# Keys of six running streams turned in 32x32 blocks on VectorE, their scores by matmuls on small parts of the array

## The chip, the core and the metric

One Trainium2 chip, of which one core is used. The metric is the device time of one execution in microseconds, from the first to the last instruction with what the runtime counts around it. A core has TensorE (matmul, PE; its weight loads are listed as PEld), VectorE (DVE), ScalarE (ACT), GpSimd (POOL) and SyncE (SP), which here issues nearly all DMAs.

## The reference, cut to what matters

One step of a two-layer encoder in fp32: a prompt of 1024 rows and eight running streams of 16 rows each, model width 1024. Layer 0 joins a gated linear recurrence (four heads) with differential attention (four heads, two components of 64 columns each, so 128 columns a head); layer 1 is a pooling mixer; each layer ends in a ConvFFN. The change touches the attention of the running streams alone. Each of the eight streams has 2048 cached keys and values for each head, and its 16 new rows attend to those and to its own 16 new keys:

```
def probs(qa, ka):
    s = einsum('bqhd,bkhd->bhqk', qa, ka) * scale + bias
    return softmax(where(visible, s, neg))
attn = probs(q[..., :64], k[..., :64]) - lam * probs(q[..., 64:], k[..., 64:])
out = einsum('bhqk,bkhd->bqhd', attn, v)
```

For one stream the scores are a 128 x 2064 matrix: 4 heads x 2 components x 16 rows down, keys across.

## The kernel before, in words

The kernel is one long program in which side work, written as a Python generator, is woven into main work: `weave(main, side, per_step, skip)` takes `per_step` steps of the side for each step of the main, after the first `skip`. A step is what lies between two `yield`s. Every engine works through its own instructions in order; the framework adds the waits between engines and gives out buffers, among them eight PSUM banks of 2 KB a partition (`bank`) shared by all. It can also place an instruction earlier than the text has it.

Stages in order of time: column groups of the input projection with prompt attention beside them; then, from about 357 to 597 us, four feature-major groups (`fm_group`, tile pfm, 18 steps each) and the token-major group "ag" (`tm_group`, tile ptm, 18 steps) with the running streams (`streams`) beside them at R3 = 1.924 from the sixth step on (S3 = 5); then six stream steps alone (S4) and the recurrence (`hgrn`) with stream steps at R4 = 0.553; then the output projection's first columns with the rest of the streams at R5 = 1.669. The ConvFFN of layer 0, the pooling mixer and the ConvFFN of layer 1 fill the rest to 2590 us.

`streams` goes through n = 0, 1, 2, ...; group n is 256 cached keys, b = n // 8 is the stream and g = n % 8 the group in it. For each n it has up to four steps:

- `key_load` of group n + 1 (512 KB, three buffers kraw), and `key_tr` of group n: eight 128x128 transposes on TensorE into two banks (pk), copied to kt by VectorE and ScalarE, one each.
- `key_scores` of group n - 1: four matmuls, one for each head, each with 32 columns of queries (two components of 16; `qbd` has zeros where a component does not look) against 256 keys, into one bank (pss), which is copied to Sx. The four heads lie in four strips of 32 output partitions. Behind a stream's last group follows its `softmax`.
- `prob_tr` of group n - 11: two transposes of probabilities (ppt), copied to pT, and the load of 512 KB of values (vraw, three buffers).
- `prob_values` of group n - 12: eight matmuls of 32 columns of probabilities against 128 columns of values, summed in one bank (pos) over the whole stream. The stream's own 16 keys and values go through psn and vn.

So a step in which n is below 11 has the first two parts alone. In the profile a matmul in fp32 of 128x32 weights has two records, a transpose one, and their weight loads likewise. Projection matmuls are three for each product, over operands split into two parts; in pfm each streams 384 columns.

After the fm stage `more_act` makes ScalarE take all of the streams' copies.

## Time and profile before

| | |
|---|---|
| median of 3 runs | 2591.48 us (2591.3 to 2594.12) |
| the profiled execution's own time | 2592.14 us |
| its span, first to last instruction | 2590.4 us |
| mean granted TensorE clock | 0.982 of full |
| instructions | 45462 |
| moved by DMA | 323.78 MB, 125 GB/s over the span |

The rows that the prediction uses stand in a section of their own below. An engine's busy time in a stretch is compared with the stretch's length; where TensorE's records overlap, its busy time counts them once. In the timeline neighbouring records of one kind are merged, with the start of the first and the length to the end of the last.

### The profile page before, as it was taken

The numbers are of one execution on the slowest core, as the hardware profiler recorded it, in microseconds if no ns is written. First come the engines' busy times: TensorE is split into PE (matmuls) and PEld (weight loads), VectorE is DVE, ScalarE is ACT, GpSimd is POOL, SyncE is SP. The second block draws the span as 40 slices with busy tenths as digits, with TensorE's granted clock in tenths as the row PEclk, the third lists the DMA queues.
The fourth block names the chain that finished last, engine by engine and source line by source line (L and its number), as shares of the span: only waits on it lengthen the run. The fifth ranks groups of instructions, "written<-read, shape, count | busy, mean of one in ns | idle before, by whom it ended". The sixth has DMA issues, their size and how long they took to land. (4 is left out here: it accounts for less than half of the span.)

```text
span 2590.4 us, 45462 instructions
## 1 busy us (share of the span) xinstructions
PE 2505.6 (97%) x18090; PEld 2304.9 (89%) x18090; DVE 1550.1 (60%) x2706; ACT 1074.3 (41%) x2176; POOL 954.8 (37%) x729
## 2 busy tenths in 40 slices
PE   8999999998999998999999999989899999999997
PEld 8999988786879998999999788879899999987886
DVE  3377754337984685555554665788745555556557
ACT  2255555354772443444444111266344444431113
POOL 1210111005652355555554121245555555531222
PEclk9999999998999999999999999999999999999999
DMA  5634347777766213222224422223322222252222
GB/s 170 198 111 133 84 151 247 234 247 225 246 217 233 81 62 130 77 77 77 70 75 137 163 79 96 77 61 111 114 91 76 70 72 75 77 210 91 95 79 82
DMA packets 279539, 323.78 MB, mean 125 GB/s; under 512 B 46380, under 2 KB 209781, under 8 KB 279328
## 3 DMA queue, kind: packets, MB, share of 16 engines
q1 hardware_dynamic: 276901, 319.26, 37.9%
q8 instruction: 142, 2.33, 0.4%
q10 hardware_dynamic: 2426, 1.63, 0.3%
q14 instruction: 70, 0.57, 0.1%
HBM read 244.38 MB, written 76.46 MB: 124 GB/s over the span
## 5 line engine op out<-in xcount | busy, mean ns | idle before, releaser
L157 POOL TENSOR_TENSOR lo<-raw,hi 128x512 fp32r<-128x512 f32 x362 | 515.1, 1436 | 1094.4 <-ACT hi L156 971.4
L144 PE MATMUL pu<-xh,hi 128*128 128x288 f32 (+1 forms) x1504 | 458.9, 305 | 4.6 <-DVE xl L157 2.5
L144 PE MATMUL pu<-xl,hi 128*128 128x288 f32 (+1 forms) x1504 | 458.0, 304 | 1.4 <-DVE xl L157 1.4
L156 ACT CAST hi<-raw 128x512 fp32r<-128x512 f32 x378 | 230.4, 620 | 548.8 <-PE pu L144 273.7
L144 PE MATMUL pu<-xh,lo 128*128 128x288 f32 (+1 forms) x1504 | 457.9, 304 | 0.0
L144 PE MATMUL pd<-lo,gh 128*128 128x512 f32 x792 | 315.7, 399 | 0.0
L144 PE MATMUL pd<-hi,gh 128*128 128x512 f32 x792 | 314.7, 398 | 0.4 <-ACT gh L156 0.4
L144 PE MATMUL pd<-hi,gl 128*128 128x512 f32 x792 | 310.6, 393 | 0.4 <-DVE gl L157 0.4
L144 PEld LDWEIGHTS pu<-xh,hi 128*128 128x128 f32 x1504 | 285.0, 190 | 5.0 <-DVE xl L157 2.8
L144 PEld LDWEIGHTS pu<-xl,hi 128*128 128x128 f32 x1504 | 285.3, 190 | 1.7 <-DVE xl L157 1.7
L1452 DVE TENSOR_TENSOR acc<-acc,pd 128x512 f32<-128x512 f32 x330 | 216.2, 682 | 116.9 <-PE pd L144 116.4
L144 PEld LDWEIGHTS pu<-xh,lo 128*128 128x128 f32 x1504 | 285.0, 189 | 0.0
L144 PE MATMUL ptm<-hi,xh 128*128 128x256 f32 x720 | 209.3, 291 | 4.6 <-ACT hi L156 4.6
L144 PE MATMUL ptm<-hi,xl 128*128 128x256 f32 x720 | 201.8, 280 | 0.6 <-DVE xl L157 0.6
L144 PE MATMUL ptm<-lo,xh 128*128 128x256 f32 x720 | 201.8, 280 | 0.1
L1226 DVE SCALAR_TENSOR_TENSOR cv<-ext,prm,cv 128x1024 f32<-128x1024 f32 (+1 forms) x176 | 183.8, 1098 | 21.0 <-ACT cv L1223 21.0
L144 PEld LDWEIGHTS pd<-hi,gh 128*128 128x128 f32 x792 | 149.1, 188 | 38.4 <-ACT gh L156 1.0
L144 PEld LDWEIGHTS pd<-hi,gl 128*128 128x128 f32 x792 | 148.9, 188 | 37.4 <-DVE gl L157 1.3
L144 PEld LDWEIGHTS pd<-lo,gh 128*128 128x128 f32 x792 | 149.2, 188 | 33.4
L144 PEld LDWEIGHTS ptm<-hi,xh 128*128 128x128 f32 x720 | 136.3, 189 | 7.8 <-ACT hi L156 5.7
L144 PEld LDWEIGHTS ptm<-lo,xh 128*128 128x128 f32 x720 | 136.3, 189 | 0.9 <-DVE lo L157 0.4
L144 PEld LDWEIGHTS ptm<-hi,xl 128*128 128x128 f32 x720 | 135.8, 189 | 0.8 <-DVE xl L157 0.8
(331 smaller groups left out, 5770.7 us busy)
## 6 DMA issues: line engine op xcount, KB each, us to landing
raw<-in_ffn_w_up SPq DMA_DIRECT2D x88, 512.0 KB
kraw<-in_cache_k SPq DMA_DIRECT2D x64, 512.0 KB
vraw<-in_cache_v SPq DMA_DIRECT2D x64, 512.0 KB
g_scr<-cv SPq DMA_DIRECT2D x44, 576.0 KB
graw<-g_scr SPq DMA_DIRECT2D x44, 576.0 KB
raw<-in_ffn_w_down SPq DMA_DIRECT2D x44, 512.0 KB
raw<-in_w_in_ab SPq DMA_DIRECT2D x28, 512.0 KB
x_scr<-acc SPq DMA_DIRECT2D x18, 512.0 KB
```

The source lines that it names most:

```text
L144: nc.tensor.matmul(out, a, b, start=start, stop=stop, skip_group_check=True)
L156: nc.scalar.copy(hi, src)
L157: (sub or nc.vector).tensor_tensor(lo, src, hi, ALU.subtract)
L1226: nc.vector.scalar_tensor_tensor(dst, tap[j], cw[j], dst, ALU.mult, ALU.add)
L1452: nc.vector.tensor_tensor(acc[t][:, cs], acc[t][:, cs], p, ALU.add)
```

## The change

For the first six streams (NBLK = 6) keys are no longer transposed by TensorE. `key_load` brings 512 keys (1 MB, two buffers). `key_tr` has VectorE turn every 32x32 block of 256 keys in place; within each block, keys and features change places, and blocks stay where they are. So feature block j (of four 32-column blocks of a head) for key block r (of four 32-key blocks of 128) lies on partitions 32r to 32r + 31. `block_scores` then works for 512 keys at once: for each j, r and head one matmul with 32 rows of weights, 16 or 32 columns of queries and 128 keys as the moving data, 64 in all. Row strip r writes bank r of four; the four j are summed there. j = 2 and 3 carry the second component (32 weight columns, the first 16 zero), j = 0 and 1 the first (16 columns). Four copies of 128 columns, two on ScalarE and two on VectorE, put the scores into Sx in the order of the keys. The bias on the last 128 keys becomes an operation of `softmax`.

The queries are needed four times down the partitions, one copy for each row strip: at the start VectorE repeats them (rep4), TensorE transposes them (16 transposes), ScalarE scales them into q_lo and q_hi. These two live as long as the fm stage, so that stage takes stream steps alone at its end until the sixth stream's last keys are scored. The last two streams go on as before, with one kt buffer. `key_scores` now stands ahead of `key_tr` in a round, and the "ag" group uses the buffers of `fm_group` for its output.

```diff
--- before.py
+++ after.py
@@ -39,6 +39,8 @@
 HIST = 15
 NEG = -1e30
 CHUNKS = ((0, 384), (384, 384), (768, 384))
+NBLK = 6
 LEVELS = (1, 2, 4, 8, 16, 32, 64)
 LAST = 3
 LATE = 3
@@ -306,11 +308,15 @@
             if kk == 3:
                 yield
-    def tm_group(st, name, c0, j, along=None, sub=None):
+    def tm_group(st, name, c0, j, along=None, sub=None, tags=None):
         w = load_cols(w_in, c0 + 256 * j, sub)
         cs = slice(256 * j, 256 * j + 256)
         for t0 in range(0, NT, 3):
-            sg = st.tile([128, 3, 256], F32, tag="sg", name="sg")
+            if tags:
+                sg = st.tile([128, NTOK], F32, tag=tags[t0 // 3 % 2], name="sg", bufs=1)[:, 0:768]
+                sg = sg.rearrange("p (t c) -> p t c", t=3)
+            else:
+                sg = st.tile([128, 3, 256], F32, tag="sg", name="sg")
             for tt in range(3):
                 p = bank([128, 256], "ptm")
                 for _ in tm_unit(w, t0 + tt, p):
@@ -603,47 +609,81 @@
                 nc.sync.dma_start(new[:, 512 * n + 256 * j:512 * n + 256 * j + 256], tm_scr[name][j][rows, :])
         return new[:, 0:512], new[:, 512:1024]
-    def streams(sa, sc1, coef, gb, qn, kn, more_act):
+    def streams(sa, sc1, coef, gb, qn, kn, mode):
         S, kraws, kts, pTs, po_of, r_of = {}, {}, {}, {}, {}, {}
         def q_of(h, b):
             return qbd[:, h, b].rearrange("p c q -> p (c q)")
-        def key_load(b, g):
-            kraw = sa.tile([128, 2, 512], F32, tag="kraw", name="kraw", bufs=3)
-            nc.sync.dma_start(kraw, i["cache_k"][0, b, 256 * g:256 * g + 256].rearrange("(s p) h c -> p s (h c)", p=128))
-            kraws[b, g] = kraw
+        def key_load(b, u):
+            kraw = sa.tile([128, 4, 512], F32, tag="kraw", name="kraw", bufs=2)
+            nc.sync.dma_start(kraw, i["cache_k"][0, b, 512 * u:512 * u + 512].rearrange("(s p) h c -> p s (h c)", p=128))
+            kraws[b, u] = kraw
         def key_tr(b, g):
-            kraw = kraws.pop((b, g))
-            kt = sa.tile([128, H, 256], F32, tag="kt", name="kt", bufs=2)
+            kraw = kraws[b, g // 2][:, 2 * (g % 2):2 * (g % 2) + 2, :]
+            if b < NBLK:
+                nc.vector.transpose(kraw.rearrange("p s c -> p (s c)"), kraw.rearrange("p s c -> p (s c)"))
+                return
+            if g % 2:
+                kraws.pop((b, g // 2))
+            kt = sa.tile([128, H, 256], F32, tag="kt", name="kt", bufs=1)
             for hp in range(2):
                 p = bank([128, 2, 2, 128], "pk")
                 for hh in range(2):
                     for s in range(2):
                         h = 2 * hp + hh
                         tr(p[:, hh, s, :], kraw[:, s, h * 128:(h + 1) * 128])
-                (nc.scalar.copy if hp or more_act else nc.vector.tensor_copy)(
+                (nc.scalar.copy if hp or mode.get("more_act") else nc.vector.tensor_copy)(
                     kt[:, 2 * hp:2 * hp + 2, :], p.rearrange("p h s c -> p h (s c)"))
             kts[b, g] = kt
         def key_scores(b, g):
             if g == 0:
                 S[b] = sa.tile([128, PAST + 16], F32, tag="Sx", name="Sx", bufs=2)
-            Sx, kt, c0 = S[b], kts.pop((b, g)), 256 * g
+            Sx, c0 = S[b], 256 * g
+            if b < NBLK:
+                if g % 2:
+                    block_scores(b, g // 2, Sx[:, c0 - 256:c0 + 256])
+                return
+            kt = kts.pop((b, g))
             p = bank([128, 256], "pss")
             for h in range(H):
                 nc.tensor.matmul(p[32 * h:32 * h + 32, :], q_of(h, b), kt[:, h, :], start=True, stop=True)
             if g == 7:
                 nc.vector.tensor_copy(Sx[:, c0:c0 + 128], p[:, 0:128])
                 nc.vector.tensor_tensor(Sx[:, c0 + 128:c0 + 256], p[:, 128:256], sbias[:, 0:128], ALU.add)
-            elif g % 2 and not more_act:
+            elif g % 2 and not mode.get("more_act"):
                 nc.vector.tensor_copy(Sx[:, c0:c0 + 256], p)
             else:
                 nc.scalar.copy(Sx[:, c0:c0 + 256], p)
+        def block_scores(b, u, out):
+            mode["blocks"] = (b, u) < (NBLK - 1, 3)
+            kraw = kraws.pop((b, u)).rearrange("p s (h j k) -> p s h j k", h=H, j=4)
+            ps4 = [bank([128, 4, 32], "pss") for _ in range(4)]
+            for j in (2, 3, 0, 1):
+                for gr in range(4):
+                    r = slice(32 * gr, 32 * gr + 32)
+                    for h in range(H):
+                        q = q_lo[r, h, j, b] if j < 2 else q_hi[r, h, j - 2, b].rearrange("p c q -> p (c q)")
+                        nc.tensor.matmul(ps4[gr][32 * h:32 * h + (16 if j < 2 else 32)], q, kraw[r, :, h, j, :],
+                                         start=(j == 2), stop=(j == 1), skip_group_check=True)
+            out = out.rearrange("p (s i k) -> p s i k", s=4, i=4)
+            for gr in range(4):
+                (nc.vector.tensor_copy if gr % 2 else nc.scalar.copy)(out[:, :, gr, :], ps4[gr])
         def softmax(b):
             Sx = S[b]
+            if b < NBLK:
+                nc.vector.tensor_tensor(Sx[:, PAST - 128:PAST], Sx[:, PAST - 128:PAST], sbias[:, 0:128], ALU.add)
             p = bank([128, 16], "psn")
             for h in range(H):
                 nc.tensor.matmul(p[32 * h:32 * h + 32, :], q_of(h, b), knt[:, h, 16 * b:16 * b + 16],
@@ -666,7 +706,7 @@
             for s in range(n):
                 tr(p[:, s, :], Sx[:, 256 * g + 128 * s:256 * g + 128 * s + w])
             pT = sa.tile([w, n, 128], F32, tag="pT", name="pT", bufs=3)
-            (nc.scalar.copy if g % 2 or more_act else nc.vector.tensor_copy)(pT, p)
+            (nc.scalar.copy if g % 2 or mode.get("more_act") else nc.vector.tensor_copy)(pT, p)
             if g < 8:
                 vv = sa.tile([128, 2, 512], F32, tag="vraw", name="vraw", bufs=3)
                 nc.sync.dma_start(vv, i["cache_v"][0, b, 256 * g:256 * g + 256].rearrange(
@@ -720,20 +760,35 @@
         for c in range(2):
             r = slice(64 * c, 64 * c + 64)
             nc.scalar.activation(qbd[r, :, :, c, :], pv[r], AF.Copy, scale=0.125)
+        q_lo = mode["pool"].tile([128, H, 2, NBLK, 16], F32, name="q_lo")
+        q_hi = mode["pool"].tile([128, H, 2, NBLK, 2, 16], F32, name="q_hi")
+        nc.gpsimd.memset(q_hi.rearrange("p h j b c q -> p (h j b c q)"), 0.0)
+        for h in range(H):
+            rep4 = wp.tile([128, 512], F32R, tag="wl" if h % 2 else "wh", name="rep4", bufs=8).bitcast(F32)
+            rep4 = rep4.rearrange("p (j r c) -> p j r c", j=4, r=4)
+            nc.vector.tensor_copy(rep4, qn[:, h * 128:(h + 1) * 128].rearrange("p (j c) -> p j c", j=4)
+                                  .unsqueeze(2).to_broadcast([128, 4, 4, 32]))
+            p = bank([128, 4, 128], "pn")
+            for j in range(4):
+                tr(p[:, j, :], rep4[:, j].rearrange("p r c -> p (r c)"))
+            pv = p[:, :, 0:16 * NBLK].rearrange("p j (b q) -> p j b q", q=16)
+            nc.scalar.activation(q_lo[:, h], pv[:, 0:2], AF.Copy, scale=0.125)
+            nc.scalar.activation(q_hi[:, h, :, :, 1, :], pv[:, 2:4], AF.Copy, scale=0.125)
         yield
         oscs = {}
         for n in range(8 * NS + 23):
             b, g = divmod(n, 8)
-            if n < 8 * NS:
-                if n + 1 < 8 * NS:
-                    key_load(*divmod(n + 1, 8))
-                key_tr(b, g)
-                yield
             if 1 <= n <= 8 * NS:
                 key_scores(*divmod(n - 1, 8))
                 if g == 0:
                     softmax(b - 1)
+                yield
+            if n < 8 * NS:
+                if n % 2 == 0 and n + 2 < 8 * NS:
+                    key_load(*divmod(n // 2 + 1, 4))
+                key_tr(b, g)
                 yield
             m = n - 11
             if m >= 0 and m // 8 < NS:
@@ -974,7 +1029,8 @@
                     yield
-    st = pool_of(x1_s, "st_tm", 3, side="right")
+    st_s = ctx.enter_context(ExitStack())
+    st = pool_of(st_s, "st_tm", 3, side="right")
     at_s = ctx.enter_context(ExitStack())
     ac = pool_of(at_s, "at_const", 1)
     sbias = ac.tile([128, 144], F32, name="sbias")
@@ -1029,18 +1085,22 @@
               side, R2)
         new = load_new()
         drain(side)
+    st_s.close()
     sc1 = pool_of(at_s, "sc1", 1)
     ss = pool_of(at_s, "ss", 1)
-    more_act = []
-    running = streams(ss, sc1, coef, gb, *new, more_act)
+    mode = {"blocks": True}
+    running = streams(ss, sc1, coef, gb, *new, mode)
     next(running)
     with ExitStack() as fm_s:
         stf = pool_of(fm_s, "st_fm", 1)
+        mode["pool"] = pool_of(fm_s, "qblk", 1)
         weave(chain(fm_group(stf, 0, "q"), fm_group(stf, 512, "f"), fm_group(stf, 256, "q"),
-                    fm_group(stf, 768, "f"), tm_group(st, "ag", 1536, 1)), running, R3, S3)
+                    fm_group(stf, 768, "f"), tm_group(stf, "ag", 1536, 1, tags=("fs", "lf"))), running, R3, S3)
         first_block = load_first_block()
+        while mode["blocks"]:
+            next(running)
     x1_s.close()
-    more_act.append(True)
+    mode["more_act"] = True
     early = {}
     def load_heads(t, ot):
@@ -1070,7 +1130,7 @@
         for _ in range(S4):
             next(running)
         weave(hgrn(hg, hc, *first_block, early_heads), running, R4)
-    more_act.clear()
+    mode["more_act"] = False
     xh, xl = x_parts(ctx)
     cst = pool_of(ctx, "cst", 1, side="right").tile([128, NF, 18], F32, name="cst")
```

## Rows read from the trace of the kernel before

**Rows 1.** Page, engines: busy us (share of the span), instructions.

```profile
PE 2505.6 (97%) x18090; PEld 2304.9 (89%) x18090; DVE 1550.1 (60%) x2706; ACT 1074.3 (41%) x2176; POOL 954.8 (37%) x729
```

**Rows 2.** Windows: stretch, us, busy (instructions) by engine, clock, DMA share, GB/s.

```profile
357.00:597.00 240.00, 240.00 (x2260) 195.50 (x2262) 91.57 (x170) 108.18 (x168) 22.28 (x18) 1.00 0.77 244
367.00:405.00 38.00, 38.00 (x308) 30.88 (x308) 16.32 (x29) 15.86 (x27) 4.37 (x4) 1.00 0.83 282
380.00:390.00 10.00, 10.00 (x82) 7.76 (x84) 3.49 (x6) 2.15 (x5) 0.00 (x0) 1.00 0.97 351
450.00:550.00 100.00, 100.00 (x950) 80.14 (x949) 36.03 (x67) 44.72 (x69) 5.20 (x5) 1.00 0.75 232
597.00:772.00 175.00, 162.61 (x1802) 133.02 (x1798) 156.40 (x321) 119.21 (x342) 110.22 (x129) 0.94 0.69 231
800.00:850.00 50.00, 50.00 (x429) 50.00 (x428) 12.41 (x50) 8.24 (x15) 10.10 (x8) 1.00 0.52 189
```

**Rows 3.** Timeline, TensorE, first stage: start us, us, instruction, count.

```profile
440.24 0.38 PE L153 MATMUL ppt<-ident,Sx 128*128 128x128 f32 x2
440.55 0.64 PE L687 MATMUL pos<-vraw,pT 128*32 128x128 f32 x16
441.12 0.44 PE L144 MATMUL pfm<-xh,hi 128*128 128x384 f32 x1
...
442.79 1.03 PE L153 MATMUL pk<-ident,kraw 128*128 128x128 f32 x8
443.76 0.64 PE L636 MATMUL pss<-kt,qbd 128*32 128x256 f32 x8
444.33 0.44 PE L144 MATMUL pfm<-xh,hi 128*128 128x384 f32 x1
444.61 0.34 PE L144 MATMUL pfm<-xl,hi 128*128 128x384 f32 x1
444.79 0.34 PE L144 MATMUL pfm<-xh,lo 128*128 128x384 f32 x1
```

**Rows 4.** Groups by line, 357:597: busy us, mean ns, idle before.

```profile
L626 DVE COPY kt<-pk 128x512 f32<-128x512 f32 x47 | 32.4, 690 | 66.3 <-PE pk L153 63.5 <-issue 2.2 <-ACT lf L383 0.4
L641 DVE COPY Sx<-pss 128x256 f32<-128x256 f32 x18 | 7.6, 423 | 12.9 <-PE pss L636 9.9 <-PE ppt L153 2.6
```

**Rows 5.** Timeline, TensorE, the 27 ns from 440.545 to 440.572.

```profile
440.55 0.32 PE L687 MATMUL pos<-vraw,pT 128*32 128x128 f32 x4
```

**Rows 6.** Timeline, TensorE, products on new values, 16 rows by 32.

```profile
453.95 0.42 PE L687 MATMUL pos<-vn,pT 16*32 16x128 f32 x8
454.31 0.55 PE L153 MATMUL pk<-ident,kraw 128*128 128x128 f32 x3
```

**Rows 7.** Timeline, TensorE, where two kinds of 32-column products meet.

```profile
652.07 0.30 PE L687 MATMUL pos<-vraw,pT 128*32 128x128 f32 x2
652.10 0.23 PE L144 MATMUL psc<-qk 128*32 128x32 f32 x2
652.13 0.30 PE L687 MATMUL pos<-vraw,pT 128*32 128x128 f32 x1
```

**Rows 8.** Groups by line and shape, VectorE, whole span.

```profile
L653 DVE TENSOR_REDUCE mx<-Sx 128x1 f32<-128x2064 f32 x8 | 18.4, 2299 | 0.3
L378 DVE TENSOR_SCALAR ks<-ks,lbt 128x1152 f32<-128x1152 f32 x4 | 3.3, 816 | 1.5 <-ACT ks L377 1.5
```

**Rows 9.** DMA issues, 450:550: count and KB each.

```profile
kraw<-in_cache_k SPq DMA_DIRECT2D x17, 512.0 KB
```

**Rows 10.** Timeline, TensorE, where stream steps run alone.

```profile
594.85 1.09 PE L153 MATMUL pk<-ident,kraw 128*128 128x128 f32 x8
597.38 1.09 PE L153 MATMUL pk<-ident,kraw 128*128 128x128 f32 x8
```

**Rows 11.** Waits of SP's queue, 450:550: us, times, longest us.

```profile
SPq L672 <- PE pos L687: 36.8, 14, 4.2
```

**Rows 12.** Tile vraw: idle time of the engine before it, us, times.

```profile
  DMA vraw<-in_cache_v: 1.5, 1
```

## The prediction

> **What bounds the kernel now.** I read the page's busy line first, then stages by windows, then groups by line and shape, then TensorE's own timeline, then the transfers. The busy line has TensorE at 97% and no other engine above 60% [rows 1]: the reader is to see that work taken off TensorE can shorten the span, if the stage it stands in is TensorE's. The windows say which it is [rows 2]. From 357 to 597 us (column groups of the input projection with the running streams woven in; 90 projection steps, 1.924 stream steps for each after the first five) TensorE is busy 240.00 of 240.00 us at full clock, VectorE 91.57, ScalarE 108.18, and the transfers hold 0.77 of the DMA engines. From 597 to 772 us (the recurrence) VectorE is at 156 of 175 us and TensorE has gaps: TensorE time saved there is worth little. The six changed streams fall into the first stage: 163 stream steps are taken there, one for the set-up, 24 for groups n = 0 to 11, then four for each n, so the old kernel ends it two steps into n = 46, where the sixth stream ends at n = 48.
>
> **What is removed.** A group is 256 keys. On TensorE it costs eight transposes (pk) and four score products (pss, eight records). In the timeline [rows 3] pk starts at 442.79 and pss at 443.76: 0.97 us for eight. Two transposes (ppt to pos, 440.24 to 440.55) take 0.31, so one is (0.97 - 0.31)/6 = 0.11 us and 0.09 us is the emptying of the array before a product of another shape. From pss to the projection behind it is 0.57 us, and that product's successor comes 0.28 us later instead of 0.18: 0.10 us to get back. So a group is 0.97 + 0.57 + 0.10 = 1.64 us, and 512 keys, the new unit, 3.28 us. Off the path go the kt copies, one of 0.69 us on VectorE for each group [rows 4] and one on ScalarE.
>
> **What the 64 small products cost** is the question; no row of before uses the array in rows and columns at once with more than one row strip. What rows show: pos (16 records of 128 columns) and pss (8 of 256) both last 0.57 us [rows 3], so the time goes by the columns in one of four column strips, not by the number of instructions: 4 x 128 or 2 x 256 columns are 4 x 0.11 = 0.44 us, and 0.13 us is filling. Four strips start within 27 ns of each other [rows 5]. The 16x32 products on the new values, a 32x32 tile, do two rounds of 128 columns from 453.95 to 454.31, 0.36 us = 2 x 0.11 + 0.14 [rows 6]: small tiles are not slower. And pos records start between the last psc records of the line in front (652.07 pos, 652.10 psc, 652.13 pos) [rows 7]: a product for a free part of the array passes one that waits for its own. So I expect the 16 tiles to run side by side. A tile gets four products of two records, 8 x 0.11 = 0.88; with 0.13 filling, 0.10 return, and 0.13 for the 16 starts (four took up to 27 ns, so 16 up to about that), a unit is 1.24 us. Bounds: 1.11 without the start term; 32 rounds, the four row strips one after another, 32 x 0.11 + 0.23 = 3.75. I take 1.24, by the 32x32 row and the passing row. Gain over 24 units: 24 x (3.28 - 1.24) = 49 us. Serial: 24 x (3.28 - 3.75) = -11.
>
> The rule that speaks against it: the Trainium skill, "TensorE: Matmul & The Clock Gate", "Wait, 56ns, not 53.3ns?", says that start-to-start does not fall below about 25 ns however few the columns. Estimated by it, 128 records would be 3.2 us and a unit 3.4, no gain. The row has four records inside 27 ns in four column strips, so it does not hold across strips; whether it does across row strips no row here shows. The same page, "Packing small matmuls", gives 10.6 for 16 tiles instead of 16; an estimate by it is 128 x 0.11 / 10.6 + 0.23 = 1.56 us a unit and a gain of 41 us.
>
> **What is added elsewhere.** VectorE turns 1024 columns in place for each group. The nearest row at one element at a time is the maximum (2299 ns for 2064, 1.11 ns each, so 1.14 us); the kt copy out of PSUM has 1.35 ns each (1.38 us); the fast form is 816 ns for 1152 (0.73 us) [rows 4, 8]. I take 1.15; the ends are 0.73 and, at half speed, 2.3. The score copies become two of 128 columns on VectorE for a unit where one of 256 (0.42 us) stood [rows 4]: +0.1 a group at most. VectorE changes by 1.15 + 0.1 - 0.69 = +0.56 us a group. In steady state a group comes every 5.7 us (17 key loads, nearly 18, in 100 us) [rows 9] with 36.03/17.5 = 2.06 us of VectorE [rows 2]; afterwards 2.6 of about 4.7, 55%. Behind a turn stand, in VectorE's order, copies of z and pT; they wait at most one turn, TensorE has other banks meanwhile, and pT is needed a group later. At 2.3 us VectorE is at 80% and I charge 10 us. The score products wait for turns issued two stream steps earlier, and for four PSUM banks of eight: pos holds one and the projection one or two, so it just fits. Cost nothing, covered by one or two projection steps; without cover about 1 us a unit, 24 us.
>
> The set-up adds 16 transposes, 16 x 0.11 = 1.8 us, and four copies of 512 columns on VectorE, at most 0.69 each by the kt row; TensorE sits behind each in turn for what its own 0.44 us do not cover. 3.5 us in all. The rest (scaling on ScalarE, clearing on GpSimd) stands beside the first steps.
>
> After the stage, stream steps run alone until the sixth stream's keys are scored: seven steps, 1.75 groups. Uncovered groups took 2.53 us in the old kernel (pk at 594.85, then 597.38) [rows 10]; now about the time of their 1 MB, 2.9 us at the 360 GB/s below, so 5 us. They are missing at the far end, where TensorE is full [rows 2]: two products on probabilities less for 3.5 groups, some 3.5 us back. Net +1.5. The recurrence gets one softmax and 1.75 key groups less, -1. Single buffering of kt for the last two streams costs nothing, its readers being issued before the next transposes.
>
> **Transfers** become the second limit. 0.77 x 240 = 185 us of full transfer time stand in the stage [rows 2]. TensorE's demand after the change is 240 - 46.5 x 0.5 x 2.04 + 3.5 = 196 us: 94%. In the early part (367 to 405, keys only) it is worse: 0.83 x 38 = 31.5 us of transfers against 38 - 11 x 1.02 = 27 us of TensorE. The best 10 us stretch has 351 GB/s at 0.97 [rows 2], about 360 when full. Key loads become 1 MB, two buffers, issued when the products of the unit before last are through, two groups (9.4 us) ahead of need; SP's queue holds values behind them: 2 MB take some 5.8 us, so both arrive in time if nothing else is queued, and fm_scr stores (576 KB) and the 512 KB weight pieces are at times. Today SP waits for buffers that pos has to free (36.8 us in 100) and TensorE waited for values once, 1.5 us [rows 11, 12]: slack that is spent now. I charge 4.5 us for the early part and 5.5 later, 10 together; bounds 0 and 30.
>
> **Sum.** The profiled execution took 2592.14 us (span 2590.4 and 1.7 around it); -49 + 3.5 + 1.5 - 1 + 10 = -35 gives 2557. The median of the runs shown is 2591.48, 0.7 lower, so 2556.5.
>
> **Rivals.**
> 1. The stage becomes the transfers'. For: 94% demand, bursts, one queue in order. Against: TensorE hardly ever waits for a transfer today. If 0.85 is all that bursts let through: 185/0.85 = 218 us instead of 196, 22 us lost instead of 10: 2569, and up to 2577 at the bound of 30.
> 2. Row strips do not run side by side. For: no row shows two at once. Against: the passing of a waiting product. Half together is 16 x 0.11 + 0.23 = 2.0 us a unit, gain 31, time 2575. Wholly serial loses 11 instead of winning 49: 2617, slower. It decides where a unit passes 3.28 - 14/24 = 2.7 us, the other charges included.
> 3. Issue, not columns, sets the rate, the other side again: pos has 0.57/16 = 36 ns a record; were that a limit, 128 would be 4.6 + 0.23 us, 24 x 1.55 = 37 us slower, 2643. Against it pss, 71 ns a record in the same time [rows 3]. By the 25 ns that the Trainium skill's page "TensorE: Matmul & The Clock Gate" states (section as above) it would be an estimated 2610.
> 4. The work only changes its queue: turns at half speed hold VectorE 80% of the time and the products behind them, 10 us, 2567.
>
> **How the numbers follow.** Forecast 62% (2544 to 2567, from units of 1.11 to 1.63 us, the latter with the 0.13 of the starts paid for each of the four parts j, and 0 to 15 us of waits, the two upper ends seldom together), rival 1 17%, rival 2 half 6% and serial 5%, rival 3 5%, rival 4 5%. The range 2542 to 2578 takes in all but the slow cases and a little of rival 1. Two tenths of a per cent, 5 us, is what a measurement here can tell from no change. Faster: 62 + 17 + 6 + 5 = 90, less 2 for several charges at once, 88%; slower 10 less 1, 9%; same, what was taken off, 3%.
>
> **What would show it.** The score products: 128 records of 128 columns in about 1.2 us, overlapping across row strips (right), or in steps of 32 (rival 2) or evenly spaced (rival 3). VectorE's turn at 1.15 us. The stage some 40 us shorter with the DMA share near 0.9; TensorE's waits named kraw, vraw or the turn would speak for rival 1. The recurrence and all behind it should keep their lengths within 5 us. Wrong would be a unit over 2.7 us, or TensorE gaps of more than 15 us in the stage.

## The result and the profile after

The changed kernel is slower: 2614.1 us median (2609.1 to 2614.3) against 2592.8 (2591.3 to 2594.6) of the kernel before on the same chip, ratio 1.0076 [1.0064, 1.0088]. The forecast was 2556.5. The profiled execution took 2613.88 us (span 2611.8), 21.7 more than that of before, where 35 less were forecast: 56 us are to be explained.

The busy line of the page after, against [rows 1]: TensorE is busy 13 us less, in a longer span.

```profile
PE 2492.8 (95%) x20410; PEld 2302.8 (88%) x20410; DVE 1567.0 (60%) x2735; ACT 1052.7 (40%) x2160; POOL 966.2 (37%) x730
```

Windows of the kernel after: woven stage, steps alone behind it, recurrence (columns as in [rows 2]).

```profile
357.00:600.00 243.00, 222.05 (x4339) 190.98 (x4338) 113.42 (x189) 86.70 (x152) 25.28 (x20) 0.95 0.73 240
600.00:622.00 22.00, 16.36 (x373) 10.88 (x371) 10.49 (x23) 10.52 (x22) 6.28 (x10) 0.69 0.78 261
622.00:786.00 164.00, 148.92 (x1658) 121.22 (x1656) 149.30 (x310) 109.01 (x319) 104.62 (x121) 0.97 0.68 223
```

The reader is to see three things. TensorE, busy 240.00 of 240.00 us in [rows 2], now stands idle 21 us in the stage. Its mean granted clock there is 0.95 instead of 1.00: some 24 us at the 1.2 GHz level, which cost 12. And the DMA share has not risen. The stretches between landmarks (first pfm, last ptm, first psc, last psc, first pu; times of the TensorE timelines) tell where the 21.4 us of span are, beside what the prediction's terms make of them:

| stretch | before | after | measured | forecast |
|---|---|---|---|---|
| up to the stage | 357.6 | 358.1 | +0.5 | 0 |
| woven stage | 236.7 | 242.1 | +5.4 | -33.9 (-47.4 + 3.5 + 10) |
| steps alone | 7.3 | 21.4 | +14.1 | +3.4 (5 - 1.6) |
| recurrence | 164.5 | 164.3 | -0.2 | -4.5 with the next |
| from there to the ConvFFN | 129.9 | 131.3 | +1.4 | |
| the rest | 1694.4 | 1694.5 | +0.1 | 0 |

In the stage, time less idle time less half of the time at half clock is what TensorE's work would take at full clock: 236.7 before, 242.1 - 21 - 12 = 209 after. So 27.5 us of work went (forecast 43.9), and 33 us of waiting and slow clock came (forecast 10).

The longest of TensorE's waits in the stage (357 to 600; us in all, times, longest): behind a turn, then behind copies that VectorE or ScalarE made late.

```profile
PE pss L677 <- DVE kraw L630: 5.7, 1, 5.7
PE pfm L146 <- DVE z L372: 3.2, 1, 3.2
PE ppt L155 <- ACT pT L709: 2.8, 1, 2.8
PE pss L677 <- DVE pT L709: 2.1, 1, 2.1
```

What one block takes: TensorE's timeline of an undisturbed one.

```profile
417.26 0.64 PE L727 MATMUL pos<-vraw,pT 128*32 128x128 f32 x16
417.84 0.96 PE L677 MATMUL pss<-kraw,q_hi 32*32 32x128 f32 x57
418.52 0.28 PE L677 MATMUL pss<-kraw,q_lo 32*16 32x128 f32 x1
...
418.64 1.07 PE L677 MATMUL pss<-kraw,q_lo 32*16 32x128 f32 x62
419.64 0.44 PE L146 MATMUL pfm<-xh,hi 128*128 128x384 f32 x1
419.92 0.34 PE L146 MATMUL pfm<-xl,hi 128*128 128x384 f32 x1
```

417.84 to 419.64 is 1.80 us, and 0.10 to get back (the next projection product comes 0.28 us later instead of 0.18): 1.90 a unit, not 1.24.

VectorE's groups in the stage (busy us, mean ns, then the idle time before them), and its waits in one stretch:

```profile
L630 DVE STREAM_TRANSPOSE kraw<-kraw 128x1024 f32<-128x1024 f32 x48 | 58.6, 1232 | 73.0 <-DMA kraw<-in_cache_k 68.5 <-PE pfm L146 4.5
L391 DVE TENSOR_TENSOR lf<-z,lf 128x1152 f32<-128x1152 f32 x4 | 5.4, 1358 | 24.3 <-ACT z L390 24.3
```

```profile
443.32 1.36 DVE L391 TENSOR_TENSOR lf<-z,lf 128x1152 f32<-128x1152 f32 x1 [1.22 <-ACT z L390]
444.72 1.02 DVE L372 COPY z<-pfm 128x384 f32<-128x384 f32 x2
451.75 2.37 DVE L630 STREAM_TRANSPOSE kraw<-kraw 128x1024 f32<-128x1024 f32 x2 [6.02 <-DMA kraw<-in_cache_k]
454.05 0.39 DVE L709 COPY pT<-ppt 128x256 f32<-128x256 f32 x1
```

TensorE's timeline over the same stretch:

```profile
445.33 0.45 PE L146 MATMUL pfm<-xh,hi 128*128 128x384 f32 x1 [3.20 <-DVE z L372]
...
446.17 0.53 PE L146 MATMUL pfm<-xh,hi 128*128 128x384 f32 x1
446.49 0.53 PE L146 MATMUL pfm<-xl,hi 128*128 128x384 f32 x1
...
449.43 0.34 PE L146 MATMUL pfm<-xh,lo 128*128 128x384 f32 x1
...
454.49 0.96 PE L677 MATMUL pss<-kraw,q_hi 32*32 32x128 f32 x57 [2.15 <-DVE pT L709]
```

Read the two together. VectorE stands behind the gates' subtraction (L391), and the copies of z queued behind it come late: TensorE is idle 3.20 us. Then its products start 0.32 us apart instead of 0.17: the lower clock level, until 449. Then VectorE stands 6.02 us before a turn whose keys have not landed, pT comes behind the two turns, and TensorE is idle again. The copies do not run long; they stand in line.

### The profile page after: what moved, and what is told of

Read it like the earlier page. It is cut to its first block, busy times and chain, and to the rows that moved or that the text cites. A ratio compares the mean times of both kernels' runs of the same rounds, so it can differ in the third digit from the quotient of the medians.

```text
span 2611.8 us, 49981 instructions
## 1 busy us (share of the span) xinstructions
PE 2492.8 (95%) x20410; PEld 2302.8 (88%) x20410; DVE 1567.0 (60%) x2735; ACT 1052.7 (40%) x2160; POOL 966.2 (37%) x730
## 5 line engine op out<-in xcount | busy, mean ns | idle before, releaser
L159 POOL TENSOR_TENSOR lo<-raw,hi 128x512 fp32r<-128x512 f32 x362 | 528.4, 1473 | 1095.7 <-ACT hi L158 977.7
L1286 DVE SCALAR_TENSOR_TENSOR cv<-ext,prm,cv 128x1024 f32<-128x1024 f32 (+1 forms) x176 | 185.0, 1105 | 28.5 <-ACT cv L1283 28.5
```

The lines of the kernel that those rows point to most:

```text
L159: (sub or nc.vector).tensor_tensor(lo, src, hi, ALU.subtract)
L1286: nc.vector.scalar_tensor_tensor(dst, tap[j], cw[j], dst, ALU.mult, ALU.add)
```

## The experiments

Theory A: the turns stand in VectorE's order ahead of copies, before their keys have landed; that makes the gaps, and the clock falls behind them. Rival B: the turns' own 1.23 us. Rival C: the transfers set the pace. Edits are to the changed kernel; half-clock time is that at the 1.2 GHz level, and ratios are to the kernel before.

**late_turns.**
```
-  turn of 256 keys in each of the two steps before a block
+  if g % 2: both turns in the step just before it
```


> Both VectorE turns of a 512-key unit are issued in the step just before the unit's block of scores, instead of one in each of the two steps before it; nothing else changes, and the load is asked for where it was. Theory A (a turn stands in VectorE's order before its megabyte of keys has landed; the evacuations queued behind it come late, TensorE idles, and its clock falls after it): VectorE's wait for key loads falls from 68.5 us to under 30, TensorE's gaps of over 0.3 us between 357 and 600 from about 20 us to under 10, the stretches at half clock from some 24 us to under 10, and the time from 2614 to 2585-2600. Rival B (the turns' own 1.24 us on VectorE hold the evacuations): two turns now stand back to back, 2.5 us, so the gaps stay or grow, 2614-2625. Rival C (the stage goes at the rate of the transfers): no change, 2610-2617, with VectorE still waiting about 68 us for key loads.

2615.2 us, 1.0082 [1.0065, 1.0100]. The edit did not reach VectorE: the framework had put the turns back to where they stood.

```profile
453.14 2.37 DVE L633 STREAM_TRANSPOSE kraw<-kraw 128x1024 f32<-128x1024 f32 x2 [6.25 <-DMA kraw<-in_cache_k]
```

It is the same wait as at 451.75 above, and all 48 turns stand where they stood among VectorE's other instructions; nothing is tested by it.

**small_turn.**
```
-  nc.vector.transpose(kraw as 128x1024, in place)
+  nc.vector.transpose(kraw[:, 0, 0:32], kraw[:, 0, 0:32])
```


> VectorE turns only 32 of each turn's 1024 columns, so a turn keeps its place and its wait for the key load but loses nearly all of its 1.24 us (the scores are those of unturned keys: left out is 31/32 of the turning). Theory A: the wait is what hurts, so TensorE's gaps and half-clock stretches stay, and the time stays within 2605-2615. Rival B (the 1.24 us themselves hold the evacuations): 48 x 1.2 us come off VectorE, the gaps of about 20 us go, with the half-clock stretches, and the time falls to 2580-2595. Rival C: no change and VectorE's wait for key loads grows by about the time that the turns lose, to some 120 us.

2614.4 us, one run. B falls in the form forecast: the turns' work is gone, and TensorE still stands idle 16.4 us in the stage, with the same 24 us at half clock. The stage was 4.7 us shorter, the recurrence behind it 6 longer. VectorE's waits, 357 to 600:

```profile
DVE kraw L630 <- DMA kraw<-in_cache_k: 76.8, 18, 7.9
```

**strip_order.**
```
-  for gr in range(4): for h in range(H):
+  for h in range(H): for gr in range(4):
```


> In the block of 128 records the order is quarter of channels, head, row strip instead of quarter, row strip, head, so that neighbouring records lie on the four different row strips. If the block takes 1.6-2.0 us (forecast 1.24) because records on one row strip are not all side by side, spreading neighbours over the strips shortens the block to about 1.2-1.4 us, worth 0.6 x 23 = 14 us: 2600. If neighbours are limited by their issue alone (128 starts at one pace), the block stays at 1.6 us from first to last start and the time at 2610-2616. If neighbours that share a column strip serialize, nothing changes either, or the block gets longer where the heads were what ran side by side.

2603.9 us, one run. The block did not change: 1.61 us from first to last start in both, so the order of neighbours does not matter. The 10 us are not from it: the recurrence took 156.0 us instead of 164.3 and the half-clock time in the stage was 14 us instead of 24. With one run that stays unexplained.

**probe.**
```
+  ahead of each block of streams 1 to 5 a part of it, for
+  stream 0 the whole: 2 heads | 2 row strips | 64 columns
+  | 1 row strip | 1 head
```


> Ahead of each block of streams 1 to 5 stands a part of the same block, overwritten by it: two heads only, two row strips only, two of four sub-columns (64 columns a record), one row strip only, one head only; for stream 0 the whole block once more. Length of the part from first to last start, against 1.6 us for the whole: (a) a limit on starts, 12.6 ns a record: two heads 0.8, two row strips 0.8, half the columns 1.6, one strip or head 0.4; (b) all 16 tiles side by side at 0.2 us a record of 128 columns: two heads and two strips 1.6, half the columns 0.8, one strip or head 1.6; (c) row strips two at a time: two heads 1.6, two row strips 0.8, half the columns 0.8, one strip 0.8, one head 1.6; (d) column strips two at a time: two heads 0.8, two row strips 1.6, one strip 1.6, one head 0.8.

Timeline of three parts (two heads from 410.19, half the columns from 512.54, one strip from 574.66), each with the start of the full block behind it, but for the second, where the change of row form (32x64 to 32x128) marks it:

```profile
410.19 0.67 PE L679 MATMUL pss<-kraw,q_hi 32*32 32x128 f32 x32
410.65 0.68 PE L679 MATMUL pss<-kraw,q_lo 32*16 32x128 f32 x32
411.08 1.01 PE L679 MATMUL pss<-kraw,q_hi 32*32 32x128 f32 x58
```

```profile
512.54 0.80 PE L679 MATMUL pss<-kraw,q_hi 32*32 32x64 f32 x60
...
513.73 0.29 PE L679 MATMUL pss<-kraw,q_hi 32*32 32x128 f32 x1
```

```profile
574.66 0.64 PE L679 MATMUL pss<-kraw,q_hi 32*32 32x128 f32 x16
575.12 0.51 PE L679 MATMUL pss<-kraw,q_lo 32*16 32x128 f32 x12
575.36 0.32 PE L679 MATMUL pss<-kraw,q_hi 32*32 32x128 f32 x5
575.45 0.29 PE L679 MATMUL pss<-kraw,q_lo 32*16 32x128 f32 x4
```

From the first start of the part to that of the block behind it: whole block (128 records) 1.56 us, half the columns 1.2, two heads or two row strips (64) 0.89, one strip or one head (32) 0.7. The last figure is not the length of its part: the block behind starts at 575.36, ahead of the part's last four records. Those are the last of eight rounds (a round is one record in each of the four tiles) and start at 575.45, 0.79 us behind the first, 0.11 a round; eight rounds take 0.9. So four tiles and eight tiles alike do their eight rounds in 0.9 us, 0.11 each: the rate of the prediction, side by side. With sixteen tiles the records start 12.2 ns apart on average, in this order of strips and in that of strip_order, and the eight rounds take 1.56: as if 16 x 0.89 / 1.56 = 9 tiles worked. None of the four accounts fits: (b), (c) and (d) each want 1.6 for two heads, for two strips or for both, and (a) wants 1.6 for half the columns and 0.4 for one strip. Which resource it is stays open; each record also has a weight load of its own (20410 of each on the busy line), and no run varied these by themselves. The Trainium skill's 10.6 of 16, stated for 512 columns ("TensorE: Matmul & The Clock Gate", "Packing small matmuls"), which the prediction set aside, was nearer than 16.

**half_block.**
```
-  for j in (2, 3, 0, 1):
+  for j in (2, 0):
```


> Half of each block is left out (two of the four quarters of the channels: 64 records instead of 128; the scores lack those channels), all else stays. If the block's 2.0 us lie on the path in full (the first term of the forecast that went wrong), 24 x 0.8 to 1.0 = 19-24 us go: 2590-2596. If what is saved on TensorE only turns into waiting for late keys, under 8 us go: 2606-2614.

2600.0 us, 1.0026 [1.0014, 1.0039]: 14 us less, between the two forecasts. In the stage all of it shows (242.1 to 220.5 us), but the recurrence behind it grew to 176.4 us, with 41 us at half clock instead of 10. The block's length was on the path. At this still faster pace TensorE stood idle 18.4 us in the stage, not more than the 21 of the kernel after, with the same 24 us at half clock, and the DMA share rose to 0.81.

**turn_after.**
```
+  with tc.issue_after(last copy of the unit before):
       nc.vector.transpose(...)
```


> Each VectorE turn is issued behind VectorE's last copy of the previous unit's scores, so that in VectorE's order it can no longer stand ahead of copies that are due before its keys have landed; loads, blocks and steps stay. Theory A (turns waiting in front of evacuations): VectorE's wait for key loads falls from 68 us to under 35, TensorE's gaps over 0.5 us between 357 and 600 from some 20 us to under 12, and the time to 2595-2606. Rival C (the transfers set the pace of the stage): the wait moves to TensorE's blocks, 2609-2617. A third way, B2 (late keys hold the blocks themselves, not the evacuations): also 2609 or more, since nothing arrives earlier.

2613.7 us, 1.0083 [1.0068, 1.0099]. The edit did what it says (VectorE's waits, first row), and the time did not move: the wait went to TensorE (its waits, other rows).

```profile
DVE kraw L630 <- DMA kraw<-in_cache_k: 9.3, 4, 5.7
```

```profile
PE pss L677 <- issue: 11.1, 6, 3.8
PE pss L677 <- DVE kraw L630: 7.4, 1, 7.4
```

Part of what stands as "issue" is the turn, as VectorE's row and TensorE's show:

```profile
452.70 2.36 DVE L630 STREAM_TRANSPOSE kraw<-kraw 128x1024 f32<-128x1024 f32 x2
```

```profile
455.16 1.08 PE L677 MATMUL pss<-kraw,q_hi 32*32 32x128 f32 x52 [1.85 <-issue]
```

The turn, now behind the copies, ends at 455.06, and the block that TensorE had come to starts 0.1 us later.

**b3_buffers.**
```
-  kraw bufs=2, vraw bufs=3, load one unit ahead
+  kraw bufs=3 (kt in one of them), vraw bufs=2, two ahead
```


> A third 1 MB buffer of keys (place made by taking one of the three buffers of values and by laying kt into a key buffer), so that each unit's load is asked for one unit earlier, two units ahead of its block; turns keep the order that the framework gives them. Theory A and B2 (the keys come late since only two buffers exist): the first gap at 382 (5.8 us) and its half-clock stretch go, VectorE's wait for keys falls under 35 us, the time to 2590-2602. Rival C: the transfers are the pace, the wait only moves: 2609-2617. If the two buffers of values are too few, TensorE waits for values instead and the time rises above 2614.

2608.3 us, 1.0050 [1.0033, 1.0066]. Loads came a unit earlier and the turns moved up with them: VectorE still waited 61.3 us for keys, where under 35 were forecast.

**b3_after**: both edits.

> Third key buffer with loads asked for one unit earlier (as in b3_buffers) and turns issued behind the previous unit's last copy (as in turn_after) together. Theory A, amended by the runs before: lead alone left VectorE waiting 61 us for keys, since the turns only moved up with the loads; order alone moved the wait to TensorE's blocks; both together leave neither, so the time comes near that of the kernel without key loads: 2597-2604, VectorE's wait for keys under 15 us, no TensorE gap in front of a block over 1.5 us. Rival C (the rate of the transfers, whatever their lead): within 4 us of b3_buffers, 2605-2612.

2610.1 us, 1.0061 [1.0039, 1.0083]. No turn but the first waited for a load any more, and the stage was hardly shorter (240.1 us, 18.9 idle); the time lies where rival C had it, not theory A. So the first form of theory A falls: the wait in VectorE's order is not by itself what costs the time. What TensorE's blocks waited for, and the longest of these waits, in the middle of a block (two others, in front of blocks, end 0.1 us behind a turn, as above):

```profile
PE pss L677 <- issue: 9.2, 5, 4.1
```

```profile
397.79 1.02 PE L677 MATMUL pss<-kraw,q_lo 32*16 32x128 f32 x56
402.89 0.61 PE L677 MATMUL pss<-kraw,q_lo 32*16 32x128 f32 x6 [4.08 <-issue]
```

The records of the block's last six products wait for nothing that the engines show. The transfers have, within that gap, a packet of the instruction queue (window 400.5 to 401.6: packets, MB, share of the engines):

```profile
q1 hardware_dynamic: 701, 0.36, 108.2%
q8 instruction: 1, 0.02, 5.5%
```

It landed at 401.55, 1.3 us before TensorE went on.

**stay** and **stay_again.**
```
+  units 2 to 23: no load, the two first buffers again
```


> The key loads of the six streams are left out but for the first two units, whose two buffers the later turns and blocks use again and again (the scores are those of the same keys): no turn waits for a transfer, and 22 MB less are moved; turns, blocks, copies and steps stay. Theory A: TensorE's gaps over 0.5 us between 357 and 600 fall to under 5 us and the half-clock stretches there go, so that what is left above the forecast is the block itself (about 0.75 x 23 = 17 us); the last projection product at 572-582 instead of 600, the time 2580-2592. Rival B (turns and block copies on VectorE hold the rest, whatever arrives): the gaps stay near 20 us and the time above 2605.

> The run without the six streams' key loads once more, timed over several runs: its first time was a single one (2598.9). If the key transfers' lateness is worth some 15 us, the median is 2595-2603; if the single run was a lucky one, 2606 or more.

2598.9 us (one run), then 2596.9, 1.0012 [1.0002, 1.0022]: the loads are worth 17 us, less than the 22 to 34 that theory A first had. In the stage of stay_again (359 to 583) 8.6 us idle, clock 0.98; in that of stay, the same kernel, 10.0 idle, clock 0.96:

```profile
359.00:583.00 224.00, 215.37 (x4336) 185.35 (x4334) 115.18 (x189) 85.39 (x148) 23.25 (x18) 0.98 0.49 156
583.00:602.00 19.00, 14.52 (x370) 9.29 (x369) 9.29 (x22) 10.13 (x22) 6.25 (x9) 0.82 0.86 300
```

Rival C in its plain form fails by other runs: with all loads the share is 0.73 in the kernel after, and half_block's stage ran at 0.81. But this run takes lateness and traffic away together and does not part them.

**rate.**
```
-  R3 = 1.924
+  R3 = 2.01
```


> The stream steps per projection step of this stage go from 1.924 to 2.01, so that the last blocks of the sixth stream are issued within the woven stage instead of after it, alone. If the 21.5 us from the last projection product to the start of the recurrence (forecast 12) are stream steps without cover, about 8 to 10 us of them go and the time falls to 2603-2607. If the late keys set the pace of the stage (theory A in its strong form, or rival C), the steps only move their waiting into the stage: 2611-2617.

2605.4 us, 1.0056 [1.0039, 1.0073]: the steps alone fell from 21.4 to 12.5 us, the stage rose to 250.6, and the recurrence fell to 158.0. The number is the one forecast, the way to it is not: stage and steps together kept their length (263.5 us before the edit, 263.1 behind it), so the steps only moved into the stage. In the profile the gain is the recurrence's 6.3 us, with the same 1661 TensorE records in it, and no run says why.

**nblk5.**
```
-  NBLK = 6
+  NBLK = 5
```


> Five streams instead of six take the new way (the sixth has TensorE's transposes and 256-key products), so that no steps stand alone between the stage and the recurrence for its sake. The woven stage gets some 3.5 units x 1.3 us = 4-5 us longer, but the 14 us that the time from the last projection product to the recurrence grew by (7.3 to 21.5) go: 2602-2607 if the tail is a loss of its own; 2612 or more if its time only comes back elsewhere.

2607.6 us, 1.0056 [1.0041, 1.0071]. The steps alone are back at 6.9 us, for 4 us more of stage and 3 of recurrence; the time lies at the upper end of the first forecast.

**comb** (turn_after, strip_order, rate) and **rate_b3_after**:

> Turns behind the copies of the previous unit, the row strips innermost in the block, and 2.01 stream steps for each projection step, together. Theory A: the gains add where they are of different kinds (tail about 8, order of turns about 10, order of the block 0 to 5): 2590-2600. Rival C: no more than the tail's gain, 2603-2608.

> b3_after with 2.01 stream steps for each projection step, so that the sixth stream's last blocks lie inside the woven stage. If the uncovered tail and the late keys are two separate losses, as theory A has it, the 8 us of the rate run come on top of what b3_after gains: 2589-2597, even with the kernel before. If the tail's 8 us are the same time as the keys' (steps pulled in only wait), no better than b3_after.

2622.1 us, 1.0107 [1.0068, 1.0145], and 2614.3, 1.0083 [1.0067, 1.0099]. Both forecasts missed: the gains did not add. Gaps over 0.5 us each from 357 to 625 came to 29.2 us in rate_b3_after and 28.5 in rate, against 24.9 in b3_after and 24.7 in the kernel after: more steps in the stage made more gaps, whatever the order of the turns.

**pool_lf.**
```
-  nc.vector.tensor_tensor(lf, z, lf, ALU.subtract)
+  nc.gpsimd.tensor_tensor(lf, z, lf, ALU.subtract)
```


> The gates' last subtraction (L391), for which VectorE stands still 24 us in four waits with copies of pT and z queued behind it, goes to GpSimd; nothing else changes. If this wait of VectorE is what holds TensorE in the gaps that stay without key loads (442, 452, 524-528), the gaps over 0.5 us between 357 and 600 fall by 5 us or more, with the half-clock stretches behind them, and the time to 2602-2609. If the keys' lateness covers the same time, no change: 2610-2616.

2621.7 us, 1.0107 [1.0083, 1.0130], slower. VectorE's next copies into z and sg now wait for GpSimd to be done with the same buffers (waits, 357 to 610):

```profile
DVE z L372 <- POOL lf L391: 16.5, 3, 10.8
...
DVE sg L329 <- POOL lf L391: 10.4, 1, 10.4
```

**nblk5_all** (nblk5, b3_after, pool_lf): 2608.7 us, 1.0060 [1.0045, 1.0075], as nblk5 alone and above both forecasts.

> Five streams the new way, a third key buffer with loads two units ahead, turns behind the previous unit's copies, and the gates' subtraction on GpSimd. If tail, late keys and VectorE's wait for the gates are three losses of their own (some 10, 4 and 5 us), they add to 2592-2598, even with the kernel before; if they overlap, 2600-2606.

**old_products.**
```
-  if b < NBLK: turns on VectorE, blocks
+  if b < 0:    (TensorE's transposes, 256 keys, as before)
```


> New loads (1 MB, two buffers), new order of the steps, set-up of the small queries and one buffer of kt as in the changed kernel, but keys turned by TensorE and scored 256 at a time as before, for all streams. If the loading scheme is at fault by itself, TensorE waits for keys here too, and the time is 2600-2615. If it hurts only at the faster pace and through VectorE's order, the time is that of before plus the set-up: 2593-2599.

2607.0 us, 1.0048 [1.0032, 1.0065] (2599.5 to 2608.2). New loads and order without the new products, by windows: stage, steps alone, recurrence.

```profile
359.00:602.00 243.00, 239.37 (x2248) 199.29 (x2246) 87.80 (x165) 107.90 (x172) 23.37 (x18) 1.00 0.74 240
602.00:609.00 7.00, 7.00 (x98) 5.44 (x98) 2.99 (x9) 4.53 (x11) 4.26 (x7) 1.00 0.87 289
609.00:784.00 175.00, 164.58 (x1660) 132.52 (x1658) 153.16 (x312) 112.92 (x324) 105.72 (x123) 0.87 0.65 217
```

Where TensorE has its old work, the same loads leave it 3.6 us idle in the stage and no half clock: the loading scheme does not hurt beside the old products. (The old pace and the turning on TensorE come back together here, so the run does not say which of them it is.) It reaches the recurrence 7 us later, and the rest is the recurrence's 10 us more, at clock 0.87 against 0.94 in [rows 2]. TensorE waits no more there than before (10.4 us, 12.1 before), so the 10 us are not waits for loads; what lowered the clock is open. Over the runs, more half-clock time there mostly goes with a longer recurrence (156 us with 7, 164 with 10 to 24, 175 with 44).

**stay_rate**: stay and rate.

> No key loads for the six streams but two units (the scores are those of the same keys), and 2.01 stream steps for each projection step, so that neither late keys nor the steps after the stage stand in the way: a bound on what better loading and a better pace could bring. If the two losses add, 2588-2593, no faster than the kernel before: then the blocks at their measured length, with the waits for the gates and the softmax, leave no gain to win. If they overlap, 2596-2602. A gain of 10 us or more over the kernel before (under 2582) would say that the change only lacks a better loading scheme.

2581.8 us, 0.9957 [0.9942, 0.9972], the only kernel faster than before, but no usable one, since it scores the same keys again. Against rate (2605.4) the loads are worth 24 us, and against stay_again (2596.9) the rate is worth 15 where it gave 9 with the loads: the two losses are not independent. Of the 15 us, 8.5 are the recurrence's (158.4 instead of 166.9), as in rate. The time lies just under the 2582 from which, by the expectation, the change lacks only a better loading scheme; no run here found that scheme. Stage (TensorE idle 7.6 us) and steps alone:

```profile
357.00:581.00 224.00, 216.36 (x4481) 186.32 (x4479) 116.13 (x193) 85.27 (x152) 22.68 (x18) 0.99 0.52 165
581.00:595.00 14.00, 8.99 (x219) 5.68 (x219) 9.17 (x17) 8.63 (x15) 6.09 (x9) 0.95 0.85 292
```

## Why the prediction was wrong

Its reading of the old kernel held: TensorE bounded that stage, and 27.5 us of its work went. Its sum failed in three steps.

**"A unit is 1.24 us": measured 1.90, 16 us too little over 24 units.** The step that failed is "So I expect the 16 tiles to run side by side": the 0.88 us of columns with 0.13 for the starts measured 1.56 (probe). The rows that it rested on showed four tiles at a time, and four or eight do run side by side; sixteen do not. Rival 2 had the size (half together, 2.0 us a unit) with the wrong reason, and would still have come out at 2575. The removed side fits (23.25 units at 3.28 less 1.90, less 3.5 for the set-up, make 28.6 us; 27.5 went), the turn was right (1.15 forecast, 1.23 measured), and rivals 3 (36 ns a record; 12.2 measured) and 4 fell.

**"Cost nothing, covered by one or two projection steps" and "10 together" for the transfers: measured 33 us of idle time and half clock, 23 too little.** This was the decisive step. The forecast took the cover of the old kernel for granted in the new one. The chain of the gates (L383 to L391), the softmax, the key loads, the casts had fitted behind a TensorE that was always full, and with the same loads they nearly still do beside the old products (3.6 us idle in old_products). In the new kernel now one, now another of them ends last: VectorE waits 24.3 us for the gates, where it waited 5.9 in the stage of before. That the shorter work of TensorE alone brings this about is not shown: half_block has less work still and no more idle time. What else came with the new way (turns in VectorE's order, blocks that want a whole megabyte turned, four banks at once) was not tested apart from the pace. The prediction named the price without cover (24 us), rated it at nothing, and left the clock out: 12 us. Of the 33 us, 8.6 idle and about 5 of half clock remain without the key loads in stay_again, 10.0 and 8.5 in stay. So some 14 to 19 hang on the loads. Rival 1 had the right resource and the wrong mechanism: the share stayed at 0.73 over the stage (0.76 from 367 to 405), below the 0.85 it needed and the 0.77 of before. Whether the lateness of each load or its traffic does it is not settled: with lead and order mended (b3_after) TensorE still stood idle 18.9 us, about 5 of it in waits that end behind a packet of instructions (4.1 and 1.0) and 6 in front of blocks whose turn, now behind the copies, was not through.

**The steps alone, "net +1.5": measured +14.** They took 21.4 us, 5.6 of them idle and 13.7 at half clock. 3.5 us are idle since a copy of that part stands in ScalarE's order behind a cast whose weights have not come; the other 2.1 are the wait at 611.5 of the last section. TensorE's and ScalarE's rows for the first:

```profile
603.52 0.44 PE L155 MATMUL ppt<-ident,Sx 128*128 128x128 f32 x2
607.46 1.08 PE L727 MATMUL pos<-vraw,pT 128*32 128x128 f32 x16 [3.50 <-ACT pT L709]
```

```profile
606.52 0.62 ACT L158 CAST hi<-raw 128x512 fp32r<-128x512 f32 x1 [3.58 <-DMA raw<-in_w_out_ab]
607.04 0.37 ACT L709 COPY pT<-ppt 128x256 f32<-128x256 f32 x1
```

And what the early work was to give back later (-4.5) did not come: the recurrence kept its length, which with the same work varied by 6 us and more between runs (rate, strip_order).

Together: 16 + 23 + 11 + 6 (4.5 not given back and 1.3 lost behind it) + 0.5, some 56. The forecast's own sign of error, over 15 us of gaps in the stage, is what came; a slower result was given 9%, all of it to rivals about the array, none to the loss of cover.

## What to carry over

Work taken off a full engine is worth its time only as long as the chains beside it still fit. Before counting the gain, add up for each in-order queue what it does in one unit at the new pace, with its waits, and price the first stretch that no longer fits, the clock included. The key loads, a megabyte each with two buffers held through load, turn and product, cost 17 us here; one unit more of lead won some 6 of them back (b3_buffers). Moving a wait by order or to another engine (turn_after, pool_lf) moved the loss with it: find first what comes next in line. And a gain that lies in a stretch which the edit did not touch (rate, strip_order) is not yet one of the edit.

## What the runs showed of the hardware

- 32x32 products with 128 columns, eight rounds: on four tiles some 0.9 us (32 records), on eight 0.89 (64), on sixteen 1.56 (128). So eight tiles cost no more than four, sixteen are hardly better than eight (12.2 ns a record against 13.9), and 64 columns a record still take 1.2 us for 128. TensorE does not start its records strictly in the program's order: the block's first start ahead of its forerunner's last (the probe's rows from 575.36).
- TensorE seems to run out of instructions at times. In the kernel after, turn_after, b3_after and stay_rate, thirteen of its waits for nothing shown ("issue") between 357 and 625 us, 0.7 to 4.1 us long, ended 1.3 to 1.6 us behind the landing of a 16 KB packet of the instruction queue; two are of the kernel after (404.3 and 611.5). The queue has 160 packets after the change and 142 before, and in the stage of before TensorE never waits. From 357 to 625 us 37 of these packets land in the kernel after and 19 in that of before; half_block has 26 and none of these waits, the probe 43 and thirteen, each ending 1.2 to 1.5 us behind a landing. The Trainium skill ("Runtime: NRT & Kernel Launch", "Instruction fetch mechanics") calls such a refill mostly hidden; read so, with blocks close together, these traces disagree. It is read from times alone: no run varied the packets by themselves.
- In place, VectorE turned 128x1024 in 32x32 squares in 1.23 us, 1.20 ns a column.
